# A hybrid transformer layer on one core: the MLP's two matrix products by seven block products of Strassen instead of eight

## The chip, the core and the metric

The kernel runs on one NeuronCore of a Trainium2 chip. TensorE (PE in the profile; PEld is its weight load) multiplies matrices into PSUM, VectorE (DVE), ScalarE (ACT) and GpSimd (POOL) work on elements, and SyncE (SP) issues nearly all DMA transfers, in the order in which they stand in its queue. The metric is the time on the device of one execution, in microseconds (us); smaller is better. Everything is float32. TensorE multiplies float32r operands here, so each float32 product is made of three matmuls on operands that are split into a high part (rounded) and a low part (the rest): high by high, high by low, low by high.

## What is computed

One layer over 2048 tokens of width 1024: a combined input projection, an attention group and a gated group, an output projection with residual, and at the end the squared-ReLU MLP. Only the last two lines are touched by the change:

```python
h = rms_norm(x, norm2_g[l])
f = jnp.square(jax.nn.relu(jnp.einsum('bsd,df->bsf', h, w_ff1[l])))
x = x + jnp.einsum('bsf,fd->bsd', f, w_ff2[l])
```

`h` is 2048 by 1024, `w_ff1` 1024 by 4096, `w_ff2` 4096 by 1024. Each of the two products is, in tiles of 128 by 128 by 512, 1024 tile products, and three matmuls for each: 3072 matmuls, 6144 for both.

## The kernel before

The program has four stages: a first sweep over the 16 token tiles (projections of q, k and v, and row maxima), attention, a second sweep (`sweep2`: the gated group and the output projection, whose sums are the residual that goes to DRAM as four tensors `x1_d`, named x_d in the profile), and `mlp`. All instructions go through a framework that gives each engine a list in an order of its own: it takes them by the order of the program, by the operands that they wait for and by the free buffers of their pools. So two orders matter: that of the source, and that of each engine's list. A pool gives out `bufs` buffers per tag in turn; a tile that takes a buffer waits until its last user is done.

`mlp` works on blocks of 1024 tokens (`TB`), two of them. `prep` loads a tile of 128 rows into `acc` (line 1112, kept for the whole block as the accumulator), squares it on ACT for the norm (line 1115), and transposes it on PE with `ident` (line 246); `split_ps` takes the transposed tile out of PSUM as `hh` (high, ACT line 175) and `hl` (low, DVE line 176), which stay in SBUF for the block. Then it loops over pairs of the 32 column blocks f of `w_ff1` (`CF = 2`). `load_w1` loads a block of 1024 by 128 as `w1r` (line 1071), POOL multiplies it with the norm's gain (line 1072), and `split_sb` makes `w1h` on ACT (line 168) and `w1l` on DVE (line 169). `load_w2` does the same with 128 rows of `w_ff2`. `ff1` multiplies by `gemm3` (lines 205 to 207, one line for each of the three products), applies relu on ACT (line 1096), squares on POOL (line 1097), and splits the result into `fh` and `fl`, which stay in SBUF. `ff2` multiplies these with `w2h`, `w2l` for each of eight token tiles and two halves of the 1024 output columns; DVE multiplies each PSUM bank with the row's 1/rms squared and adds it to `acc` (line 1107). After the last pair of a block `acc` goes to the output.

For the first four tiles of the first block, `prep` alternates with what is left of the second sweep (`rest`), so that PE has work while the tiles are loaded.

Of the kernel before, what the change touches and what calls it, by code (L numbers as in the profile page):

```python
# [8 lines left out]
F32 = mybir.dt.float32  # L9
F32R = mybir.dt.float32r  # L10
AF = mybir.ActivationFunctionType
ALU = mybir.AluOpType
# [51 lines left out]
class InOrder:  # L64
    """An engine whose instructions keep the order in which they are written."""
# [13 lines left out]
class Halves:  # L79
    """Two tiles of four blocks each, indexed as one of eight."""  # L80
# [11 lines left out]
class Engines:  # L92
    """The engines of a core; those named in `pinned` keep the written order."""
# [10 lines left out]
def tile_hybrid_block(  # L104
# [57 lines left out]
    def split_sb(dst_hi, dst_lo, raw, scale=None, on_pool=False):  # L162
        """dst_hi + dst_lo = scale * raw, exactly, with dst_hi rounded to float32r."""
# [14 lines left out]
    def inv_rms(dst, ssq, n):  # L178
        """dst = (ssq / n + eps) ** -0.5"""
        en.vector.tensor_scalar(dst, ssq, 1.0 / n, EPS, ALU.mult, ALU.add)  # L180
        en.gpsimd.tensor_tensor(dst, dst, expo[: dst.shape[0], : dst.shape[1]], ALU.pow)

    def inv_rms_n(pool, dst, ssq, n, name):
        """as inv_rms, by a square root, a reciprocal and a Newton step"""
# [10 lines left out]
    def gemm3(ps, pairs, by_pass=False):  # L195
        """ps = sum over (a_hi, a_lo, b_hi, b_lo) of the three products that float32 needs."""
# [17 lines left out]
    def load_x_t(pool, pst, t, nxt=2, newton=False, tag="tr", xt=None, apart=False, into=None):  # L214
        """x tile, its transposed copy split in two, 1 / rms of its rows."""
# [47 lines left out]
    # additive masks: q by k for the maximum, k by q for the scores (own block, next block)  # L263
# [23 lines left out]
    # ================= sweep 1: q, k, v and the maxima of two branches =================  # L287
    def sweep1():
        if True:
# [87 lines left out]
            def maxima(m, units):  # L377
                """units: (query view, key view, mask, column of m); the masked row maxima."""
# [62 lines left out]
            def behind(t, qn, kn, step):  # L441
                """the part of tile t that trails its projections, in steps between later ones"""
# [26 lines left out]
            def late4(t, n):  # L469
                """a share of the second branch's maxima of the group before"""  # L470
# [58 lines left out]
            def finish(pe, dve):  # L529
                """what is left of the maxima, in two parts"""  # L530
# [9 lines left out]
    # ================= attention: joint softmax over the three branches =================  # L540
    def attention(finish, xnp, xs, tpe, wu):
        with ExitStack() as st:
# [92 lines left out]
            def scores(units, msk, i):  # L635
                """units: (ks, k2, qh, q2 views, width); the exponentials, split in two"""
# [26 lines left out]
            def due(everything=False):  # L663
                """what was put off until some steps had passed"""
# [19 lines left out]
            def head_jobs(h, T):  # L684
# [5 lines left out]
                # d = 1: one bank for 512 queries in order  # L690
# [25 lines left out]
                # d = 4 and d = 16: one bank for each residue mod 4, the query 16 i + 4 c + r in column (c, i)  # L716
# [50 lines left out]
            def first_x(step):  # L767
                """of the next sweep's first tile, the part due at this step"""
# [30 lines left out]
            def weights(step):  # L799
                """of the next sweep's first weights, the part due at this step, counted from the last head"""  # L800
# [48 lines left out]
    # ================= sweep 2: u, g, spatial gating, output projection =================  # L849
# [199 lines left out]
    # ================= squared-ReLU MLP =================  # L1049
    def mlp(pst, late, rest):  # L1050
# [3 lines left out]
        CF = 2  # L1054
        with ExitStack() as st:
            new = lambda name, **kw: st.enter_context(tc.tile_pool(name=name, reuse_waits="tile", **kw))
            cp = new("f1", bufs=1)
            ap = new("f1a", bufs=1)
            rp = new("f1r", bufs=2)
            wps = [new("f1w", bufs=1)]  # L1060
            hh = [cp.tile([P, KD, 512], F32R, name="hh0")]
            hl = [cp.tile([P, KD, 512], F32R, name="hl0")]
            g2 = ap.tile([P, KD], F32, name="g2")
            nc.scalar.dma_start(g2, norm2_g[0].rearrange("(k p) -> p k", p=P))

            def load_w1(f):
# [56 lines left out]
            for t in range(4):  # L1123
                accs.append(prep(0, t))
                if rest:
                    rest.pop(0)()
# [85 lines left out]
```

## Time and profile before

| | |
|---|---|
| median of 3 runs | 2584.57 us (2583.3 to 2596.1) |
| span of the profiled execution, first to last instruction | 2579.8 us |
| what lies around the span, by the median | 4.8 us |
| PE busy | 2534.3 us, 98% of the span |
| DVE, ACT, POOL busy | 51%, 28%, 22% |
| DMA | 209.29 MB, mean 81 GB/s |
| first matmul of the MLP, last matmul's start | 1153.9 us, 2574.7 us |

The time of the profiled execution itself isn't listed apart from its span; the span stands 4.8 us (0.2%) under the median of the runs. The MLP is the stretch from 1153.9 us to the end, 55% of the span. A row of the profile that groups instructions gives line, engine, operation, output and inputs by their names in the program, their shapes, a count, and then the busy time and the mean duration of one in ns. PE's durations are of pipelined matmuls that overlap (about 390 ns each); what one costs in a stream is the distance from start to start. A row of windows gives for each stretch the busy time of each engine with the number of instructions (x), then the granted TensorE clock, the busy share of the DMA engines and what they moved. A row of the timeline gives start, duration, engine, line and operands, and in brackets how long the engine was idle before it and what it waited for.

### The profile page before, as it was taken

The numbers are of one execution on the slowest core, as the hardware profiler recorded it, in microseconds if no ns is written. First come the engines' busy times: TensorE is split into PE (matmuls) and PEld (weight loads), VectorE is DVE, ScalarE is ACT, GpSimd is POOL, SyncE is SP. The second block draws the span as 40 slices with busy tenths as digits, with TensorE's granted clock in tenths as the row PEclk, the third lists the DMA queues.
The fourth block names the chain that finished last, engine by engine and source line by source line (L and its number), as shares of the span: only waits on it lengthen the run. The fifth ranks groups of instructions, "written<-read, shape, count | busy, mean of one in ns | idle before, by whom it ended". The sixth has DMA issues, their size and how long they took to land.

```text
span 2579.8 us, 31560 instructions
## 1 busy us (share of the span) xinstructions
PE 2534.3 (98%) x12052; PEld 2105.5 (82%) x12052; DVE 1322.7 (51%) x2892; ACT 731.7 (28%) x1248; POOL 558.2 (22%) x460
## 2 busy tenths in 40 slices
PE   8999999999988999999999999999999999999999
PEld 6777777999977888878888888888788888888887
DVE  6556656777764444454343444444534444444444
ACT  5222223655662222243212121211322121121210
POOL 1000003555531122122212122221122222121210
PEclk9999996988889999999999999999999999999999
DMA  6434446655542212142111111111321111111111
GB/s 196 107 66 95 95 102 155 176 129 151 182 124 71 74 58 66 58 141 64 57 41 58 41 57 42 49 50 49 127 69 58 42 49 49 49 49 50 49 33 66
DMA packets 189175, 209.29 MB, mean 81 GB/s; under 512 B 16080, under 2 KB 151760, under 8 KB 185296
## 3 DMA queue, kind: packets, MB, share of 16 engines
q1 hardware_dynamic: 180544, 205.67, 27.9%
q10 hardware_dynamic: 8480, 1.60, 0.4%
q8 instruction: 95, 1.56, 0.3%
q14 instruction: 56, 0.46, 0.1%
HBM read 160.19 MB, written 46.99 MB: 80 GB/s over the span
## 4 chain that ended last, share of the span: by engine, by line
PE 94%; DMA 2%; DVE 2%; ACT 1%; issue 1%; POOL 0%; SPq 0%; ACTq 0%; DVEq 0%; POOLq 0%
PE ps_f L205 18%; PE ps_f L206 18%; PE ps_f L207 18%; PE ps_mm L205 8%; PE ps_mm L206 8%; PE ps_mm L207 8%; PE ps_as L74 6%; PE ps_o L74 4%; PE ps_sc L382 2%; PE ps_tr L246 2%; PE ps_mx L74 1%; PE ps_mm L74 1%; PE ps_tr L361 1%; DMA a<-at_d 0%; DMA out_dram<-acc 0%
## 5 line engine op out<-in xcount | busy, mean ns | idle before, releaser
L1107 DVE SCALAR_TENSOR_TENSOR acc<-ps_f,ss,acc 128x512 f32<-128x512 f32 x512 | 378.4, 748 | 231.3 <-PE ps_f L207 231.1
L205 PE MATMUL ps_f<-hh,w1h 128*128 128x512 f32 x1024 | 402.7, 393 | 0.2 <-ACT hh L175 0.2
L206 PE MATMUL ps_f<-hl,w1h 128*128 128x512 f32 x1024 | 402.5, 393 | 0.0
L207 PE MATMUL ps_f<-hh,w1l 128*128 128x512 f32 x1024 | 402.2, 393 | 0.0
L205 PE MATMUL ps_f<-w2h,fh 128*128 128x512 f32 x1024 | 398.8, 389 | 0.0
L206 PE MATMUL ps_f<-w2l,fh 128*128 128x512 f32 x1024 | 398.7, 389 | 0.0
L207 PE MATMUL ps_f<-w2h,fl 128*128 128x512 f32 x1024 | 398.7, 389 | 0.0
L169 DVE TENSOR_TENSOR fl<-relu,fh 128x512 fp32r<-128x512 f32 x128 | 88.6, 692 | 466.1 <-ACT fh L168 466.1
L1072 POOL TENSOR_TENSOR w1r<-w1r,g 128x1024 f32<-128x1024 f32 x64 | 122.5, 1914 | 869.3 <-DMA w1r<-in_w_ff_dram 626.6
L205 PEld LDWEIGHTS ps_f<-hh,w1h 128*128 128x128 f32 x1024 | 192.5, 188 | 43.8 <-ACT hh L175 0.5
L207 PEld LDWEIGHTS ps_f<-hh,w1l 128*128 128x128 f32 x1024 | 192.6, 188 | 43.6
L206 PEld LDWEIGHTS ps_f<-hl,w1h 128*128 128x128 f32 x1024 | 192.5, 188 | 43.0
L205 PEld LDWEIGHTS ps_f<-w2h,fh 128*128 128x128 f32 x1024 | 192.2, 188 | 42.0
L207 PEld LDWEIGHTS ps_f<-w2h,fl 128*128 128x128 f32 x1024 | 192.3, 188 | 40.0
L206 PEld LDWEIGHTS ps_f<-w2l,fh 128*128 128x128 f32 x1024 | 192.2, 188 | 38.8
L1097 POOL TENSOR_TENSOR relu<-relu 128x512 f32<-128x512 f32 x128 | 165.8, 1295 | 242.6 <-ACT relu L1096 242.6
L74 POOL TENSOR_TENSOR pl<-e,ph 128x512 fp32r<-128x512 f32 x144 | 175.5, 1234 | 160.9 <-ACT e L74 122.5
L168 ACT ACTIVATE w2h<-w2r 128x1024 fp32r<-128x1024 f32 x64 | 64.6, 1053 | 510.6 <-PE ps_f L207 508.1
L168 ACT ACTIVATE fh<-relu 128x512 fp32r<-128x512 f32 x128 | 80.9, 632 | 299.9 <-POOL relu L1097 299.9
L74 PE MATMUL ps_o<-ph,v 128*64 128x128 f32 (+3 forms) x816 | 151.1, 272 | 0.9 <-ACT nacc L74 0.9
L74 PE MATMUL ps_as<-qh,ks 128*128 128x256 f32 (+1 forms) x384 | 144.9, 384 | 0.0
L74 PE MATMUL ps_as<-q,k 65*128 65x256 f32 (+1 forms) x384 | 137.1, 369 | 0.0
(254 smaller groups left out, 4234.4 us busy)
## 6 DMA issues: line engine op xcount, KB each, us to landing
w1r<-in_w_ff_dram SPq DMA_DIRECT2D x64, 512.0 KB, 4.5
w2r<-in_w_ff_dram SPq DMA_DIRECT2D x64, 512.0 KB, 3.3
v<-v_d SPq DMA_DIRECT2D x24, 1040.0 KB, 10.4
xt<-in_x_dram SPq DMA_DIRECT2D x32, 512.0 KB, 5.5
v_d<-vt SPq DMA_DIRECT2D x16, 520.0 KB, 6.3
ks<-kt_d SPq DMA_DIRECT2D x16, 512.0 KB, 8.3
x_d<-xt SPq DMA_DIRECT2D x16, 512.0 KB, 2.6
acc<-x_d SPq DMA_DIRECT2D x16, 512.0 KB, 4.4
```

Of the source, the lines that this page charges most:

```text
L74: return self.tc.keep_in_program_order(op(*args, **kwargs))
L168: en.scalar.activation(dst_hi, raw, AF.Copy)
L169: (en.gpsimd if on_pool else en.vector).tensor_tensor(dst_lo, raw, f32(dst_hi), ALU.subtract)
L205: en.tensor.matmul(ps, ah, bh, start=(i == 0), stop=False)
L206: en.tensor.matmul(ps, ah, bl, start=False, stop=False)
L207: en.tensor.matmul(ps, al, bh, start=False, stop=(i == n - 1))
L246: en.tensor.transpose(ps[:, k - k0, :], src[:, k * P : (k + 1) * P], ident)
L361: nc.tensor.transpose(pt[:, j, :], qn[:, j * P : (j + 1) * P], ident)
L382: order[0].matmul(ps[:, j, : mk.shape[1]], qv, kv, start=True, stop=True)
L1072: nc.gpsimd.tensor_tensor(r3, r3, g2.unsqueeze(2).broadcast_to([P, KD, P]), ALU.mult)
L1097: nc.gpsimd.tensor_tensor(r, r, r, ALU.mult)
L1107: nc.vector.scalar_tensor_tensor(acc[:, cs], ps, r2, acc[:, cs], ALU.mult, ALU.add)
```

## The change

Both products are done on operands cut into 2 by 2 blocks, with Strassen's seven products of sums of blocks in place of eight products of blocks. `A_OF`, `B_OF` and `C_OF` say for each product i which blocks are added or subtracted to make its left and right operand, and into which blocks of the result it goes.

- **Norm.** `prep` now applies the norm and its gain before the products: DVE multiplies the rows by 1/rms (line 1094) and takes the transposed tile out of PSUM times the gain (line 1101), as float32 and not split, into `hT`; two DMAs write it to DRAM (`ht_d`, line 1102). 1/rms comes from POOL's power (`inv_rms`).
- **Right operands of the first product.** `h_op` reads blocks of 512 channels by 512 tokens back from `ht_d` (line 1117), DVE adds two of them (line 1120), and `split_sb` makes `bh{i}`, `bl{i}`: seven pairs that stay in SBUF for a block of 1024 tokens, one buffer each. For the second block of tokens the sums are made during the first one and kept in DRAM (`hs_d`, lines 1268 and 1132). The rows, the transposed tiles and the parts of the sums all share one tag, `raw`, of four buffers.
- **Left operands of the first product.** For each of 16 pairs j of column blocks, `load_w1` loads four blocks `w1r` (256 KB each, line 1162); `w_op` makes seven operands: five sums on POOL (tile `as`, line 1105) and seven splits on ACT and DVE (`ah`, `al`).
- **First product.** `ff1` makes seven products of 12 matmuls each (line 1198) in four PSUM banks. Some products accumulate on a bank that has been read already, so that fewer sums are left: DVE does six additions out of PSUM (lines 1209 to 1237), ACT a copy and four relus and squares.
- **Left operands of the second product.** POOL makes five sums of the four result blocks (line 1105, tiles `c`), and seven DMAs of 256 KB (line 1216) write the seven left operands, not split, to DRAM (`s_d`), for each j and each of the two blocks of tokens.
- **Second product.** Seven products in halves of the inner dimension: 14 passes (`passes`), each over 8 steps n. A step reads a left operand of 512 KB from `s_d` into `sr` (line 1304, three buffers), splits it (`s`, four buffers), does 24 matmuls into one bank (line 1316), and DVE adds the bank to one or two of the 16 accumulators `acc` (line 1326), which all stay in SBUF. The right operands `t` of a pass (four tiles; ten buffers) are made during the pass before, from one or two loads of `w_ff2` each (line 1293), a sum on POOL and a split.

```diff
+            def prep(gt):
+                tb, t = divmod(gt, NTB)
+                h = raw()
+                nc.sync.dma_start(h, x1_d[gt // 4][(gt % 4) * P : (gt % 4 + 1) * P, :])
...
+                nc.vector.tensor_scalar(h, h, ss[:, 1:2], None, ALU.mult)
...
+                    nc.vector.tensor_tensor(hT3[:, ks, :], ps, g2[:, ks].unsqueeze(2).broadcast_to([P, 4, P]), ALU.mult)
+                    nc.sync.dma_start(ht_d[tb, kh, t // 4, :, :, (t % 4) * P : (t % 4 + 1) * P], hT3[:, ks, :])
...
+            def h_sum(i, tb, kc):
...
+                        nc.sync.dma_start(r, ht_d[tb, kh, th, :, kc : kc + 2, :])
+                        parts.append(r)
+                if op is not None:
+                    nc.vector.tensor_tensor(parts[0], parts[0], parts[1], op)
+                return parts[0]
...
+            ORDER1 = (3, 2, 1, 5, 4, 7, 6)
+            early = ORDER1[:4]
+            for n, t in enumerate((4, 5, 6, 7, 0, 1, 2, 3)):
+                prep(t)
+                if rest and n % 2:
+                    rest.pop(0)()
+            h_op(ORDER1[0], 0, hop[0])
...
+            def ff1(j, tb, wops):
...
+                            nc.tensor.matmul(
+                                ps[bank], a[:, k, :], b[:, k, :], start=first and k == n == 0,
+                                stop=(k == 3 and n == 2), skip_group_check=True,
+                            )
...
+                for i in (1, 2, 6, 7):
+                    first, second, op = A_OF[i]
+                    dst = c_tile() if i < 3 else f[first]
+                    combine(dst, op, f[first], f[second])
+                    keep(i, dst)
...
+            def s_op(i, half, n):
+                r = sp.tile([P, NH, P], F32, tag="sr", name="sr", bufs=3)
+                nc.sync.dma_start(r, s_d[i, n, :, half * NH : (half + 1) * NH, :])
+                s = sp.tile([P, 2, NH, P], F32R, tag="s", name="s", bufs=4)
+                split_sb(s[:, 0], s[:, 1], r)
+                return s
...
+            def ff2(i, half, n, ts, s):
+                ps = psg.tile([P, 512], F32, tag="f2", name="ps_f2")
+                for k in range(NH):
+                    t = ts[k // 2]
+                    for m, (a, b) in enumerate(((0, 0), (0, 1), (1, 0))):
+                        nc.tensor.matmul(
+                            ps, s[:, a, k, :], t[:, b, k % 2, :], start=k == m == 0, stop=k == NH - 1 and m == 2
+                        )
+                for at, op in C_OF[i]:
...
+                    nc.vector.tensor_tensor(c, c, ps, op)
```

Three places in the engines' lists matter for what follows. The first is PE's list where the second sweep ends. Before, each pair of transposes of `prep` stands between matmuls of the projection, and the MLP's first matmul follows (`ps_mm` is the projection, `ps_tr<-ident,acc` a `prep`):

```order
L206 MATMUL ps_mm<-wol_4_8085,mh 128x512
L246 MATMUL ps_tr<-ident,acc 128x128 x4
L207 MATMUL ps_mm<-woh_4_8069,ml 128x512
L205 MATMUL ps_mm<-woh_5_8070,mh 128x512
L206 MATMUL ps_mm<-wol_5_8086,mh 128x512
```

Now the transposes are those of line 1100, and the last three of the eight tiles stand after all but two of the projection's matmuls, straight ahead of the first product (`ps_f`, line 1198):

```order
L205 MATMUL ps_mm<-woh_3_8076,ah 128x512
L1100 MATMUL ps_tr<-ident,raw 128x128 x8
L206 MATMUL ps_mm<-wol_3_8092,ah 128x512
L207 MATMUL ps_mm<-woh_3_8076,al 128x512
L1100 MATMUL ps_tr<-ident,raw 128x128 x24
L1198 MATMUL ps_f_11782<-bh_11619,ah 128x512
L1198 MATMUL ps_f_11782<-bl_11620,ah 128x512
```

So 24 transposes, of the last three tiles, have moved behind the projection. The second place is SP's list at the same point of the changed program: `raw<-x_d` loads the rows of a tile, `ht_d<-raw` stores a half of a transposed tile, `raw<-ht_d` reads a part of an operand back.

```order
L1102 DMA ht_d<-raw 512x1x128 x4
L996 DMA x_d_71<-xt 128x1024
L1089 DMA raw<-x_d_68 128x1024
L1102 DMA ht_d<-raw 512x1x128 x2
L1162 DMA w1r<-in_w_ff_dram 128x4x128
L1089 DMA raw<-x_d_68 128x1024
L1162 DMA w1r<-in_w_ff_dram 128x4x128 x3
L1102 DMA ht_d<-raw 512x1x128 x2
L1117 DMA raw<-ht_d 128x1024 x2
L1102 DMA ht_d<-raw 512x1x128 x2
L1117 DMA raw<-ht_d 128x1024
```

Where before SP issued seven loads of rows in a row, each load of a tile now stands behind the stores of the tile two before it, whose buffers it takes, and the first reads back stand behind the last stores but one pair. The third place is SP's list in the middle of the first product and at the change to the second: four loads of weights, seven stores of left operands, in turn for each j, and then the first reads of the second product.

```order
L1162 DMA w1r<-in_w_ff_dram 128x4x128 x4
L1216 DMA s_d<-c 128x4x128 x7
L1162 DMA w1r<-in_w_ff_dram 128x4x128 x2
L1216 DMA s_d<-c 128x4x128 x14
L1304 DMA sr<-s_d 128x1024 x5
L1216 DMA s_d<-c 128x4x128 x2
L1304 DMA sr<-s_d 128x1024
L1216 DMA s_d<-c 128x4x128 x5
```

Counted from the start, 4(j+3)+2 weight loads stand ahead of the first store of j through most of the loop (22 ahead of that of j = 2, 26 ahead of that of j = 3): the loads run two j and a half ahead of the stores. In the last rows five reads of `sr` have been moved ahead of the last j's stores.

More of the change, by code (lines that the diff above doesn't have):

```diff
@@ new lines, in w_op @@
+            def w_op(i, block):
+                ah = wp.tile([P, 4, P], F32R, tag="ah", name="ah", bufs=8)
+                al = wp.tile([P, 4, P], F32R, tag="al", name="al", bufs=8)
+                first, second, op = A_OF[i]
+                r = block(first)
+                if second is not None:
+                    r = wp.tile([P, 4, P], F32, tag="as", name="as", bufs=2)
+                    combine(r, op, block(first), block(second))
+                split_sb(ah, al, r)
+                return ah, al
@@ new lines, in mlp, with t_ops @@
+            f1.close()
+            acc_p = new(st, "f2a", bufs=1, side="right")
+            sp = new(st, "f2s", bufs=1)
+            tp = new(st, "f2t", bufs=1)
+            psg = st.enter_context(tc.tile_pool(name="ps_f2", bufs=6, space=PSUM, reuse_waits="tile"))
+            AHEAD = 2
+            ORDER2 = (5, 3, 2, 4, 1, 6, 7)
+            NP = NT // 2
+            NH = NFP // 2
+            accs = {}
+            def t_ops(i, half):
+                first, second, op = B_OF[i]
+                for c in range(half * NH, (half + 1) * NH, 2):
+                    parts = []
+                    for at in (first, second):
+                        if at is not None:
+                            fh, dh = nb(at)
+                            r = raw().rearrange("p (k d) -> p k d", k=2)
+                            src = w_ff2[2 * c * P : (2 * c + 4) * P, dh * 512 : (dh + 1) * 512]
+                            nc.sync.dma_start(r, src.rearrange("(k f p) d -> p f k d", f=2, p=P)[:, fh])
+                            parts.append(r)
+                    if op is not None:
+                        combine(parts[0], op, *parts)
+                    t = tp.tile([P, 2, 2, 512], F32R, tag="t", name="t", bufs=10)
+                    split_sb(t[:, 0], t[:, 1], parts[0])
+                    yield t
@@ new lines, in mlp @@
+            passes = [(i, half) for i in ORDER2 for half in range(2)]
+            steps = [(*p, n) for p in passes for n in range(NP)]
+            ss = [s_op(*steps[0])]
+            ts = list(t_ops(*passes[0]))
+            ss += [s_op(*at) for at in steps[1:AHEAD]]
+            for m, (i, half) in enumerate(passes):
+                nts, more = [], t_ops(*passes[m + 1]) if m + 1 < len(passes) else iter(())
+                for n in range(NP):
+                    at = m * NP + n + AHEAD
+                    if at < len(steps):
+                        ss.append(s_op(*steps[at]))
+                    ff2(i, half, n, ts, ss.pop(0))
+                    nts.extend([t] if (t := next(more, None)) is not None else [])
+                ts = nts
```

247 lines of the change are left out of this document (150 added, 97 removed).

## The prediction

> **What bounds the kernel now.** I read the page's head and its chain of waits first, then windows over the MLP.
>
> ```profile
> span 2579.8 us, 31560 instructions
> PE 94%; DMA 2%; DVE 2%; ACT 1%; issue 1%; POOL 0%; SPq 0%; ACTq 0%; DVEq 0%; POOLq 0%
> 1200.00:1800.00 600.00, 600.00 (x2626) 492.46 (x2625) 165.35 (x224) 31.24 (x53) 1.00 0.15 48
> 1900.00:2500.00 600.00, 600.00 (x2626) 492.44 (x2625) 159.39 (x217) 33.05 (x56) 1.00 0.15 48
> 1153.87 0.50 PE L205 MATMUL ps_f<-hh,w1h 128*128 128x512 f32 x1 [0.25 <-ACT hh L175]
> L207 PE MATMUL ps_f<-w2h,fl x1024: 387/389/476, 1202.6 to 2574.7; 128*128 128x512 f32 x171
> 1800.00:1900.00 100.00, 96.01 (x451) 78.59 (x450) 48.57 (x75) 32.34 (x52) 20.75 (x13) 1.00 0.38 122
> ```
>
> The chain is PE's. The two long windows, of the MLP's tiles alone, show PE without a gap at full granted clock: 600/2626 = 0.2285 us from matmul to matmul. 6144 of them are 1404 us of the 1421 us between the first matmul (1153.9) and the last (2574.7); the rest is 64 transposes, some 6 us, and the change of blocks in the last row. DMA is at 0.15. So in the MLP only the number of matmuls counts, as long as operands come in time.
>
> **What goes: matmuls.** Seven products of eight: first product 32 (j, block) x 7 x 12 = 2688, second 14 passes x 8 steps x 24 = 2688; 5376 in place of 6144. At 0.2285 the 768 are worth 175 us.
>
> **The price of a matmul under more DMA.** The distance isn't the same everywhere. While a `w1r` is landing, and while no DMA runs:
>
> ```profile
> 1501.00:1505.00 4.00, 4.00 (x18) 3.20 (x17) 0.69 (x1) 1.23 (x2) 0.66 (x1) 1.00 0.47 131
> 1501.04 0.40 PE L207 MATMUL ps_f<-hh,w1l 128*128 128x512 f32 x1
> 1503.85 0.39 PE L207 MATMUL ps_f<-hh,w1l 128*128 128x512 f32 x1
> ...
> 1517.00:1521.00 4.00, 4.00 (x19) 3.30 (x19) 2.17 (x4) 0.00 (x0) 0.00 (x0) 1.00 0.00 0
> 1516.82 0.39 PE L207 MATMUL ps_f<-w2h,fl 128*128 128x512 f32 x1
> 1519.54 0.39 PE L207 MATMUL ps_f<-w2h,fl 128*128 128x512 f32 x1
> ```
>
> Each pair of rows is twelve matmuls apart: 2.81/12 = 0.2342, and 2.72/12 = 0.2267. The transfer there runs at 131/0.47 = 279 GB/s of a full set of engines. The change moves far more: 11 DMAs of 256 KB per j are 2.88 MB, 10.3 us of some 19.4 at that rate; a step of the second product reads 512 KB of left operand and 12/7 x 4/8 x 512 KB of weights, 0.97 MB, 3.5 us of 5.5. So transfers run a little over half the time, and I take the middle, 0.2305: 5376 x 0.2305 = 1239 us, with 0.2267 (1219) and 0.2342 (1259) as the ends.
>
> The Trainium skill, page SBUF — State Buffer, section Who interferes with whom, says that a DMA never contends with a compute engine. By that the price would be 0.2267 whatever is moved, 20 us less. The trace doesn't bear it out here: its 0.2342 stands beside a busy DMA.
>
> **Work of the other engines in a j.** Rows by engine, shapes apart:
>
> ```profile
> L169 DVE TENSOR_TENSOR fl<-relu,fh 128x512 fp32r<-128x512 f32 x128 | 88.6, 692 | 466.1 <-ACT fh L168 466.1
> L989 DVE TENSOR_TENSOR xt<-ps_mm,xt 128x512 f32<-128x512 f32 x32 | 22.0, 686 | 26.5 <-PE ps_mm L207 26.5
> L168 ACT ACTIVATE fh<-relu 128x512 fp32r<-128x512 f32 x128 | 80.9, 632 | 299.9 <-POOL relu L1097 299.9
> L1096 ACT ACTIVATE relu<-ps_f 128x512 f32<-128x512 f32 x128 | 75.5, 590 | 191.7 <-PE ps_f L207 191.6
> L74 POOL TENSOR_TENSOR pl<-e,ph 128x512 fp32r<-128x512 f32 x112 | 143.2, 1293 | 137.5 <-ACT e L74 113.2 <-PE ps_o L74 14.9 <-PE ps_as L74 8.8
> L169 DVE TENSOR_TENSOR w1l<-w1r,w1h 128x1024 fp32r<-128x1024 f32 x64 | 79.7, 1245 | 81.6 <-ACT w1h L168 81.4
> L168 ACT ACTIVATE w1h<-w1r 128x1024 fp32r<-128x1024 f32 x64 | 67.8, 1059 | 59.3 <-PE ps_f L206 59.3
> ```
>
> Per j of 84 x 0.2305 = 19.4 us: DVE 7 x 0.69 + 6 x 0.69 = 9.0, ACT 7 x 0.63 + 9 x 0.59 = 9.7, POOL ten sums x 1.29 = 12.9. Per step of 24 x 0.2305 = 5.5 us: DVE 1.25 + half a split 0.62 + 12/7 x 0.69 = 3.0, ACT 1.06 + 0.53 = 1.6. All of it lies beside PE's matmuls, so I cost it at nothing; were that cover gone, POOL's 12.9 a j would be 413 us. Stores wait in SP's list for POOL's last sums, and weight loads are queued behind them; but those loads stand two and a half j ahead of the stores, so a wait of some 8 us there reaches nobody.
>
> **The start of the first product.** Here PE has nothing else to do, and the round trip through DRAM is on the path.
>
> ```profile
> 1137.04 0.63 PE L246 MATMUL ps_tr<-ident,m 128*128 128x128 f32 x4
> 1119.79 0.48 DVE L74 TENSOR_SCALAR m<-m,ms 128x512 f32<-128x512 f32 x1 [0.66 <-POOL ms L181]
> L1115 ACT ACTIVATE hn<-acc 128x1024 f32<-128x1024 f32 x16 | 16.9, 1058 | 15.9 <-DMA acc<-x_d 15.7
> L181 POOL TENSOR_TENSOR ms<-ms,expo 128x1 f32<-128x1 f32 x16 | 9.2, 574 | 178.4 <-DVE ms L180 158.9 <-issue 19.5
> acc<-x_d SPq DMA_DIRECT2D x16, 512.0 KB, 4.4
> x_d<-xt SPq DMA_DIRECT2D x16, 512.0 KB, 2.6
> ks<-kt_d SPq DMA_DIRECT2D x16, 512.0 KB, 8.3
> q<-qt_d SPq DMA_DIRECT2D x8, 512.0 KB, 10.3
> ```
>
> Four `raw` buffers, two for a tile, let two tiles be under way. PE's list puts the first tile's transposes just behind `ps_tr<-ident,m`, so near 1137.5. From then a pair of tiles takes a load 4.4, the square 1.06, the power and its handing over 1.2, the scaling 0.9 (twice 0.48), transposes 1.0, DVE 0.7 and SP's waits for the stores in between, near 10: loads of the third, fifth and seventh tile at about 1139, 1149, 1160, the eighth tile's transposes at 1171, its stores and the read back (4.4) near 1177, add and high part 2.3: the first product starts near 1180 in place of 1153.9, **26 us** late. What is late next are the seven operands: five sums of four reads and two plain ones of two are 24 reads through four buffers, six rounds; a round holds its buffers for landing 4.4, add 1.25, split 1.06 + 1.25, 8.0 in all: 48 us, and with the last product some 50 for the first j in place of 19.4, **31 us** more. PE's list pulls 15 matmuls of the next j ahead, -3. Together **+54**. By the landing of 2.6 (rounds of 6.2, pairs of 8) it would be near 30; by that of 8.3 (rounds of 11.9, pairs of 14) near 90. I take the row nearest in kind, 4.4: the same loads at the same place.
>
> **Two smaller seams.** At the second block of tokens each operand has one buffer, free after its product in the last j and due 16.6 us later (six products of 2.77). The last one's reads stand in SP's list behind the last stores, about 8 us after the last product (add, relu, square, four sums of 1.29); with 4.4 and a split of 2.3 that is 15: just in time, **+2** (0 to 8). Where the second product starts, left operands and weights are split into memory that the last products have just left: four splits of 1.25 on DVE after the fourth and fifth of seven products, **+4** (0 to 12).
>
> **The sum.** Start 1153.9 + 54 + 1239 + 64 transposes 6 + seams 6 + tail 5.1 (2579.8 - 2574.7) = 2464 for the span, and 4.8 around it: **2469 us**. The ends added up give 2425 and 2535; likely not all at once, 2435 to 2510.
>
> **Rivals.** A: the start is hidden and the matmuls cost what they cost now; the whole 175 us come, **2409**. For it: nothing but the short landing; against it the list of PE, with nothing behind the transposes but the products that wait for them. 10%.
>
> B: POOL bounds the first product. Its sums and DVE's subtractions run side by side, and POOL's squares show a spread that could be such a collision:
>
> ```profile
> L1097 POOL TENSOR_TENSOR relu<-relu x128: 1037/1043/1597, 1165.2 to 2532.3; 128x512 f32<-128x512 f32 x128
> ```
>
> Ten at 1.60, a tile's power 0.57 and seven DVE operations of 0.69 in series make 21.4 us a j, 2.0 more than PE's; x 32 = 64 us: **2533**. It decides from 1.9 us a sum; the mean of 1.29 speaks against it. 12%. The Trainium skill, page SBUF — State Buffer, section Who interferes with whom, says that a DVE instruction with two SBUF inputs and a GpSimd one that reads SBUF exclude each other, which is this series; the spread above agrees.
>
> C, the other side: the second product waits for its left operands from DRAM. Three `sr` buffers, each held for a landing and a split of 2.3: a step can't be shorter than (landing + 2.3)/3. At 10.3, the longest median above, it is 4.2, under 5.5; it decides from 14.3, and the whole gain is gone from about 18. At twice 10.3 a step takes 7.6, 2.1 x 112 = 237 more: **2706**. For it: DMA busy over 0.6 with 4 to 8 transfers in the queue; against it the 279 GB/s. 8%.
>
> My forecast has 70%. What a measurement here can't tell from no change is about 0.5%, 13 us. Forecast, A and most of B lie over that on the fast side: faster 0.88, same 0.05, slower 0.07. The range that holds 8 in 10 reaches into A's side and B's: 2425 to 2520.
>
> **What would show it.** Right: 5376 matmuls of the MLP, distance 0.229 to 0.232 in both products; PE idle 45 to 65 us in all between 1140 and 1235, waiting for `raw`, `bh`, `bl`; the first j some 50 us; POOL's sums near 1.3; `sr` landing in 4 to 6. Wrong: PE idle in every j (POOL over 1.9: B), in every step (landing over 14: C), or hardly at the start (A); a distance under 0.228 would say that DMA isn't what stretches it.

## The result

The changed kernel takes 2501.73 us (median of 4 runs, 2491.34 to 2507.25), the kernel before 2587.87 us beside it (4 runs, 2583.3 to 2596.1). The ratio is 0.966, 95% interval 0.963 to 0.970: 3.4% faster. The forecast was 2469 with 2425 to 2520 around it. The time lies inside, 33 us above the forecast, and the terms that make up the difference are not the ones that I was least sure of.

The head of the page of the changed kernel, and windows over its PE, to set beside the 600-us windows of before; the columns of a window are its length, PE busy with its matmuls, granted clock, DMA share, GB/s:

```profile
span 2505.5 us, 31639 instructions
```

```profile
1400.00:1500.00 100.00, 88.96 (x358) 0.93 0.90 265
1500.00:1600.00 100.00, 87.94 (x373) 0.95 0.76 227
1700.00:1800.00 100.00, 100.00 (x443) 1.00 0.54 155
1900.00:2000.00 100.00, 100.00 (x443) 1.00 0.91 326
```

From 1600 on PE is full again in both products: 443 matmuls touch each 100 us, and from start to start one takes 0.2267 us (19.04/84 in the steady j's below), less than the 0.2285 of before although DMA runs at 0.54 to 0.91 instead of 0.15. Between 1196 and 1600 it isn't full. What PE waited for at the start of the MLP (1140 to 1290), in 1250 to 1480, and in 1480 to 1680 (total us, times, longest):

```profile
PE ps_f L1198 <- ACT bh L168: 18.0, 11, 8.8
PE ps_tr L1100 <- DVE raw L1094: 15.3, 5, 5.1
PE ps_f L1198 <- DVE bl L169: 7.3, 7, 1.8
...
PE ps_f L1198 <- ACT c L1206: 7.8, 5, 2.7
PE ps_f L1198 <- DVE c L1209: 2.7, 2, 2.2
...
PE ps_f L1198 <- ACT c L1206: 9.3, 2, 8.3
```

The first three rows are the start, foreseen. The last three are not: there PE waits for a PSUM bank that ACT (line 1206) or DVE (line 1209) has not read yet.

The program is the same up to the end of the second sweep, but that end moves from run to run: the last transposes of `m` (line 246) start at 1137.4 us in the profile of before and between 1134.2 and 1149.6 in the other profiles. So the MLP is compared from those transposes to the end of the last matmul: 1437.7 us before, 1354.1 after, 83.6 less, about the 86 of the medians. In it, counted from the first matmul of each j to that of the next:

| | predicted | measured |
|---|---|---|
| last transposes of `m` to first product | 43 | 48.5 |
| j0 | 50 | 53.7 |
| j1 (with the transposes of a tile) | 17.2 | 22.5 |
| steady j | 19.4 | 19.04 |
| j9, j11 | 19.4 | 27.7, 28.7 |
| j16 (second block of tokens) | 21.4 | 33.9 |
| first product, all 32 j | 656 | 693.7 |
| second product, 112 steps | 623 | 612 |

Steady j's are j8, j12, j14, j15 and all from j17 to j30. The second product's matmuls were 0.2269 us apart before, 3072 x 0.2269 = 697 us; now it takes 612. What is left of the MLP, the start and the first product, took 1437.7 - 697 = 741 us before and takes 1354.1 - 612 = 742 now. So the first product has lost all that its 384 fewer matmuls save, 32 us of it by starting later (48.5 us behind the transposes of `m`, 16.5 before), and **the whole gain is the second product's**.

### The profile page after: what moved, and what is told of

It reads as the page before. It is cut to its first block, busy times and chain, and to the rows that moved or that the text cites. A ratio compares the mean times of both kernels' runs of the same rounds, so it can differ in the third digit from the quotient of the medians.

```text
span 2505.5 us, 31639 instructions
## 1 busy us (share of the span) xinstructions
PE 2395.5 (96%) x11284; PEld 1987.8 (79%) x11284; DVE 1467.7 (59%) x2948; ACT 938.3 (37%) x1540; POOL 844.4 (34%) x644
## 5 line engine op out<-in xcount | busy, mean ns | idle before, releaser
L1316 PE MATMUL ps_f<-t,s 128*128 128x512 f32 x2688 | 611.4, 390 | 2.2 <-DVE c L1237 1.6
L1316 PEld LDWEIGHTS ps_f<-t,s 128*128 128x128 f32 x2688 | 505.3, 188 | 108.2 <-ACT t L168 2.0
L1198 PE MATMUL ps_f<-bh,ah 128*128 128x512 f32 x896 | 360.7, 403 | 44.5 <-ACT bh L168 20.0
L1198 PE MATMUL ps_f<-bl,ah 128*128 128x512 f32 x896 | 358.3, 400 | 8.2 <-DVE bl L169 8.1
L1198 PE MATMUL ps_f<-bh,al 128*128 128x512 f32 x896 | 356.9, 399 | 0.0
L1105 POOL TENSOR_TENSOR as<-w1r 128x512 f32<-128x512 f32 x160 | 218.7, 1374 | 199.5 <-DVE al L169 138.2
L1105 POOL TENSOR_TENSOR c<-c 128x512 f32<-128x512 f32 x160 | 246.3, 1567 | 33.8 <-ACT c L1186 31.7
L1198 PEld LDWEIGHTS ps_f<-bh,ah 128*128 128x128 f32 x896 | 172.8, 193 | 92.6 <-ACT bh L168 27.2
L1198 PEld LDWEIGHTS ps_f<-bl,ah 128*128 128x128 f32 x896 | 172.9, 193 | 47.8 <-DVE bl L169 12.2
L1198 PEld LDWEIGHTS ps_f<-bh,al 128*128 128x128 f32 x896 | 173.1, 193 | 36.1
```

What stands on the lines that cost most here:

```text
L1105: nc.gpsimd.tensor_tensor(dst, a, b, op)
L1198: nc.tensor.matmul(ps[bank], a[:, k, :], b[:, k, :], start=first and k == n == 0, stop=(k == 3 and n == 2), skip_group_check=True,)
L1316: nc.tensor.matmul(ps, s[:, a, k, :], t[:, b, k % 2, :], start=k == m == 0, stop=k == NH - 1 and m == 2)
```

## How a late read stops PE

Timeline of the changed kernel in j9 (start, duration, engine, line; in brackets the idle time before, and what ended it):

```profile
1422.95 2.74 SPq L1216 DMA_DIRECT2D s_d<-c  x2
1423.51 7.21 POOL L1105 TENSOR_TENSOR c<-c 128x512 f32<-128x512 f32 x5
1425.79 0.46 SPq L1117 DMA_DIRECT2D raw<-ht_d  x1
...
1430.48 1.31 DVE L1120 TENSOR_TENSOR raw<-raw 128x1024 f32<-128x1024 f32 x1 [4.61 <-DMA raw<-ht_d]
1431.72 0.68 DVE L1209 TENSOR_TENSOR c<-c,ps_f 128x512 f32<-128x512 f32 x1
1432.45 0.51 PE L1198 MATMUL ps_f<-bh,ah 128*128 128x512 f32 x1 [2.21 <-DVE c L1209]
```

SP's list has two stores of `s_d` ahead of a read of `ht_d`; the read leaves at 1425.79 and lands near 1430.4. DVE's list has the addition that needs it (line 1120) ahead of the subtraction that frees PE's bank (line 1209), so DVE stands still for 4.61 us and PE for 2.21. The waits for ACT go back to the same kind of read, some us earlier in j9:

```profile
1416.11 1.23 DVE L1120 TENSOR_TENSOR raw<-raw 128x1024 f32<-128x1024 f32 x1 [6.90 <-DMA raw<-ht_d]
1417.96 0.60 ACT L1185 ACTIVATE c<-ps_f 128x512 f32<-128x512 f32 x1 [8.08 <-DVE c L1225]
```

An addition waits 6.90 us for its read, DVE's line 1225 stands behind it, ACT's relu waits for that line, and ACT comes so late to its copy (line 1206) that PE waits 2.70 us. And it costs more than the waits. The matmuls around them:

```profile
1425.68 0.50 PE L1198 MATMUL ps_f<-bh,ah 128*128 128x512 f32 x1 [2.70 <-ACT c L1206]
...
1427.05 0.63 PE L1198 MATMUL ps_f<-bh,al 128*128 128x512 f32 x1
1429.61 0.63 PE L1198 MATMUL ps_f<-bh,al 128*128 128x512 f32 x1
```

Behind the wait of 2.70 us the next few matmuls are still 0.23 to 0.34 apart, but from 1427.05 on 0.427 (2.56/6). In the whole first product 48 gaps (among them the transposes of eight tiles) take 62.7 us, and 110 matmuls that are 0.31 to 0.43 apart (81 of them 0.427) add 19.3; with 2.0 at its end that is nearly all of the 84.4 us by which it is longer than 32 steady j's. The Trainium skill, page TensorE: Matmul & The Clock Gate, section Part 1: The HAM clock gate (the "warmup" mystery), gives 426.7 ns for 512 columns on the gated clock, and an idle window of about 3.4 us until the gate closes; the distance agrees, but here waits of 2.2 and 2.7 us were enough. It isn't one length that decides: in e2 below a wait of 3.05 us in j9 is followed by no such matmul.

## The experiments

Each profile was taken once, so parts are compared within profiles, from the marks of the table above. How far these marks move by themselves can be seen from a1 below, which should differ from the changed kernel in nothing that counts here: the whole by 1.5 us, a single j by up to 2.6.

### Stores later in the source (e1)

```diff
                 def keep(i, r):
-                    nc.sync.dma_start(s_d[...], r...)
+                    kept.append((s_d[...], r...))
...
+                store()   # the stores of j-1, on nc.sync
                 x = product("x", 3, True)
```

> The changed kernel with one edit: the seven stores of the sums of j are written into SP's list one j later, ahead of the weight loads of the next j but one, so that no read stands behind a store whose sum POOL hasn't made yet. Theory H (head of SP's list: stores that wait for POOL hold up the reads of `ht_d` and `hs_d` behind them): j9 and j11 fall from 27.7 and 28.7 us to 19.0 to 20.5, j5 to j7 from 20.4 to 22.1 to about 19.5, j16 from 33.9 to 25 or less; the first product from 692 us to about 660; the start (j0 53.7) stays. Rival R (four `raw` buffers are too few there as well): j9, j11 and j16 stay within 3 us of what they were. Rival S (the DVE additions and the splits themselves, and POOL's sums beside them, are the price): the same, they stay.

Measured: j5 to j7 19.9 each (20.4, 20.9, 22.1), j9 21.2, j10 21.2, j11 29.8, j13 19.0 (20.4), j16 31.0; the first product 682.0, transposes of `m` to the last matmul 1340.9, 13.2 us less than the changed kernel. H expected about 660 for the first product and got a third of that fall. And the edit did not do what it says where it mattered: SP's list, as the framework orders it, has the stores and the reads of j9 to j16 in nearly the same order as before. The test had to be made on the list itself (e6 below).

### The sums of the second block at its start (e2)

```diff
-                    elif tb == 0 and j < NTB + 5:
-                        i = [i for i in ORDER1 if B_OF[i][1]][j - NTB]
-                        for kc in range(0, 4, 2):
-                            nc.sync.dma_start(hs_d[i, :, kc : kc + 2, :], h_sum(i, 1, kc))
```

> The changed kernel without the sums made ahead of time: in j8 to j12 nothing is read, added and stored in `hs_d`; the operands of the second block of tokens are made at its start as those of the first are, from two reads and an addition. All theories: j8 to j15 fall to 19.0 to 19.3 (24 us less in j8 to j13). H: j16 then has 24 reads behind the stores in SP's list and takes about what j0 took without its half-speed matmuls, 42 to 50 us instead of 33.9; net 8 to 16 us less. R: j16 is bound by the four buffers, six rounds of 8.0 us, so 48 or more, net 10 less or nothing. S: j16 about 40.

Measured: j9 22.4, j10 to j15 19.0, j8 to j15 together 17 us less; j16 51.6, 17.7 more; the whole 1353.5 against 1354.1. So the two long j's do come from the sums made ahead: all that j11 had too much, and most of it in j9, where the framework has put the first reads for j16 and DVE waits 5.73 us for one. Making the sums ahead is worth nothing: the price only stands at another place. j16 is then as long as R says, not H.

### Six `raw` buffers (e3)

```diff
-                return stg.tile([P, 1024], F32, tag="raw", name="raw", bufs=4)
+                return stg.tile([P, 1024], F32, tag="raw", name="raw", bufs=6)
-... name="c", bufs=14) ... name="w1r", bufs=6) ... name="t", bufs=10)
+... name="c", bufs=12) ... name="w1r", bufs=5) ... name="t", bufs=9)
```

> The changed kernel with six `raw` buffers instead of four (paid for with two `c`, one `w1r` and one `t` buffer). If the four buffers set the pace of the start, as predicted (pairs of tiles, 24 reads in six rounds of 8.0): three tiles are under way at once and there are four rounds, so the first product starts 8 to 14 us earlier (1182 to 1188 instead of 1196, apart from what the attention before it differs) and j0 takes 36 to 42 us instead of 53.7. If what bounds the start is the work in series (landing, square, power, scaling, transposes at half clock, the stores in SP's list): both within 5 us of what they were. H: j9, j11 and j16 stay near 27.7, 28.7 and 33.9; R: they fall to under 22, 22 and 26.

Measured: transposes of `m` to first product 40.8 instead of 48.5, as expected; but j0 51.7, j1 30.8 (22.5), j9 19.5, j10 31.0, j11 26.1, j16 34.3, the whole 1354.7. Two buffers more leave two of the later j's over 25 and j16 as it was, which is not what R expected. The run alone doesn't rule R out, since it has fewer `w1r` and `c` as well, and in j10 POOL waits 10.71 us for weights; e6 below, with four buffers, does for j9 to j11. The timeline of j0 says where the buffers' gain went:

```profile
1187.46 11.77 SPq L1117 DMA_DIRECT2D raw<-ht_d  x9
1199.29 3.04 SPq L1162 DMA_DIRECT2D w1r<-in_w_ff_dram  x3
1207.51 4.46 POOL L1105 TENSOR_TENSOR as<-w1r 128x512 f32<-128x512 f32 x2 [25.10 <-DMA w1r<-in_w_ff_dram]
1210.48 0.80 PE L1198 MATMUL ps_f<-bh,ah 128*128 128x512 f32 x1 [12.12 <-ACT ah L168]
```

With two more buffers nine reads stand ahead of the weights in SP's list; the weights leave at 1199, POOL's sums of them wait until 1207, and PE waits 12.12 us for `ah`. PE's waits for `bh` and `bl` between 1140 and 1290 fall from 25.3 us to 10.8, and waits for `ah` of 14.3 us stand in their place. In j1 PE waits 7.22 us for the transposes of the next tile, whose norm stands behind POOL's sums.

### The first eight tiles ahead (e4)

```diff
+                two = [prep(t, raw0) for t in (4, 5, 6, 7, 0, 1, 2, 3)]   # raw0: 14 buffers, given back before the operands
+                for n in range(3):
+                    next(two[n])              # load, square, scale
+                for n in range(8):
+                    if n + 3 < 8:
+                        next(two[n + 3])
+                    next(two[n])              # transposes, stores
...
```

> The changed kernel with its first eight tiles prepared through fourteen buffers of their own, in memory that the operands take over later, and written in two stages: three tiles are loaded and scaled ahead of the transposes of the first. The four `raw` buffers stay for the operands. If the pace of the tiles (buffers, and the order in which each tile's steps stand behind one another) makes the late start, the first transposes to the first product shrink from 48.8 to 25 to 32 us; j0 stays at 50 to 54. If the work itself binds (DVE 2.6 us a tile, 21 in all; reads back from DRAM), over 40.

Measured: 39.3 instead of 48.5, between the two cases, and j0 53.4. The transposes end at 1171, and then:

```profile
1172.14 6.71 SPq L1119 DMA_DIRECT2D raw<-ht_d  x4
1178.97 0.38 SPq L1173 DMA_DIRECT2D w1r<-in_w_ff_dram  x1
1184.72 0.79 PE L1209 MATMUL ps_f<-bh,ah 128*128 128x512 f32 x1 [13.90 <-ACT ah L168]
```

The same turn as in e3: one weight load leaves at 1179, behind four reads that waited for buffers. The whole is 1346.6, 7.5 us less than the changed kernel.

### Stores on ACT's queue (e5)

```diff
+                for dst, src in kept:
+                    nc.scalar.dma_start(dst, src)   # before the relu of the fourth product of the next j
```

> The changed kernel with one edit: the stores of the seven sums are issued by ACT's queue instead of SP's, in the middle of the next j, when POOL has made the sums, so that SP's list holds no wait for POOL at all. Moving them one j back on SP's own list took j9 from 27.7 to 21.2 but left j11 at 29.8 and j16 at 31.0, because SP reached them just as early. Theory H: j8 to j15 now all within 19.0 to 20.5, j16 25 to 30 (its operands' single buffers and the splits on DVE stay), the first product 692 to 655 to 665 us. Rival S (additions and splits in DVE's and ACT's lists ahead of the banks' readers, whenever the reads land): j11 stays over 25.

Measured: j3 to j11 between 21.8 and 26.4, j16 29.5, j18 24.1; first product 706.6, the whole 1366.8, 12.7 us more. ACT's own waits between 1265 and 1480 (for what, total, times, longest):

```profile
ACT c L1185 <- DVE c L1226: 22.8, 9, 4.9
ACT c L1185 <- DMA s_d<-c: 22.1, 7, 8.1
...
ACT ah L168 <- POOL c L1105: 14.8, 4, 3.7
ACT c L1206 <- POOL c L1105: 10.9, 6, 1.8
```

The framework again took the stores forward, and on ACT they hold up the relus (line 1185), the splits of the weights and the copy that frees a bank (line 1206). So a store that waits for POOL harms the list that it stands in. The marks are S's (j11 26.4, over 25), but this run does not tell H from S for SP: the first row is a wait for DVE, and both kinds wait at once.

### SP's list fixed (e6)

```diff
+            sp[0] = InOrder(tc, nc.sync)      # SP keeps the written order in the first product
...
+                    if tb == 0 and NTB <= j < NTB + 5:
+                        made = [(kc, h_sum(i, 1, kc)) for kc in range(0, 4, 2)]   # reads of ht_d first
+                    block = load_w1((j + 1) % NFP)                                # then the weights
                     ff1(j, tb, wops)                                              # stores of j-1 in it
+                    for kc, r in made:
+                        sp[0].dma_start(hs_d[i, :, kc : kc + 2, :], r)
```

> The changed kernel with SP's list fixed in the first product, from the operands of the first j on. In the two runs that moved the stores in the source only, the framework put them back: SP's list still had stores that wait for POOL ahead of the reads of `ht_d` (and, with the stores on ACT, ACT's list had them ahead of its splits). Now in each j SP has first the reads (the next tile, or four blocks of `ht_d`, and the four weights of the next j), then the seven stores of the j before, then the stores of what DVE made; at the second block of tokens all reads of `hs_d` and `ht_d` stand ahead of the stores of j15. Theory H: j8 to j15 all at 19.0 to 20.0 (in the changed kernel j9 27.7, j11 28.7), j16 20 to 26 instead of 33.9 (its first four reads land during j15), the first product 692 to 650 to 660 us. Rival S (additions and splits in DVE's and ACT's lists): j9 or j11 stay over 25, j16 over 30.

(`InOrder` keeps an engine's instructions in the order of the source.) Measured: j9, j10, j11 19.0 each, j12 19.6, j16 26.6: for j9 to j11 H's marks came true and S's did not, and j16 is 0.6 over H's range. But j5 takes 25.6, j8 27.1, j13 28.3 and j17 29.0, the first product 700.5 where H expected 650 to 660, the whole 1360.9. j8:

```profile
1408.13 2.13 SPq L74 DMA_DIRECT2D raw<-ht_d  x4
1410.32 6.76 SPq L74 DMA_DIRECT2D w1r<-in_w_ff_dram  x4
1417.13 1.23 DVE L1124 TENSOR_TENSOR raw<-raw 128x1024 f32<-128x1024 f32 x1 [9.77 <-DMA raw<-ht_d]
1418.27 0.68 DVE L1217 TENSOR_TENSOR c<-ps_f,c 128x512 f32<-128x512 f32 x1
1419.01 0.80 PE L1202 MATMUL ps_f<-bh,ah 128*128 128x512 f32 x1 [4.97 <-DVE c L1217]
```

(Lines 1124 and 1217 are the addition and a bank's reader.) Now four reads leave together at 1408 and the first pair is there only at 1417; DVE's list has the addition ahead of the bank's reader, as it had in j9 of the changed kernel, and waits. j5 is of this kind too: DVE waits 6.56 us behind the load of a tile's rows. So SP's list set which reads came late in j9 to j11. That a late read stops PE is set by DVE's list, as these rows show (no run changed that list itself).

j13 and j17 are of another kind; no read is late there. j13:

```profile
1510.86 6.68 POOL L1109 TENSOR_TENSOR c<-c 128x512 f32<-128x512 f32 x5 [3.16 <-ACT c L1190]
1519.45 1.08 DVE L169 TENSOR_TENSOR al<-as,ah 128x512 fp32r<-128x512 f32 x1 [5.52 <-ACT ah L168]
1521.19 0.80 PE L1202 MATMUL ps_f<-bh,ah 128*128 128x512 f32 x1 [5.14 <-DVE c L1214]
```

POOL's list has the five sums of results ahead of the next sums of weights (`as`); ACT's split waits 5.81 us for these, DVE's split for ACT's, and the reader of the bank (line 1214) stands behind it in DVE's list. In j17 POOL's five sums take 7.61 us and PE waits 5.51. This is what S names, splits and POOL's sums ahead of a bank's reader: S is out for j9 to j11, not as a whole.

### Tiles ahead and SP's list (f1), and the combination (f2)

f1 joins e4 and e6, with the weights of j0 ahead of the operands' reads.

> The run with SP's list fixed, and the first eight tiles prepared ahead through fourteen buffers as in the run with the tiles ahead. There the transposes ended at 1171, and the first product then stood 13.9 and 11.6 us for `ah`: the weights of j0 stood in SP's list behind reads that waited for buffers. Here they stand ahead of the operands' reads. If SP's list is what holds the start too: the first transposes to the first product 39.6 us there, 30 to 36 here, j0 of 53 to 42 to 48; the whole about 2455 to 2465. If the reads through four `raw` buffers and the additions hold j0: j0 stays at 50 to 54, the whole 2462 to 2472.

Measured: 41.0 to the first product, j0 51.9, j8 24.9, j13 27.4, j16 27.4, j17 28.1; the whole 1351.5, and 2497 us in its one timed run: above both cases. PE's first wait for a product is now

```profile
1181.10 0.79 PE L1209 MATMUL ps_f<-bh,ah 128*128 128x512 f32 x1 [17.17 <-ACT bh L168]
```

for an operand instead of for the weights of e4: with the weights ahead, the reads back are late.

f2 joins e4 and e1 and spreads the sums ahead over j8 to j15:

```diff
+                        for _ in range(2 if j < NTB + 2 else 1):
+                            i, kc = ahead.pop(0)
+                            nc.sync.dma_start(hs_d[i, :, kc : kc + 2, :], h_sum(i, 1, kc))
```

> The version that the runs point to: the changed kernel with the first eight tiles prepared ahead (first transposes to first product 39.6 us instead of 48.8), the stores a j later in the source (j5 to j11 together 8 us less), and the sums of the second block spread: two halves of an operand in j8 and j9, one in each of j10 to j15, so that two reads instead of four pass through the four `raw` buffers in a j. SP's list is left to the framework, since fixing it only moved the waits to j8, j13 and j17. If a late read that DVE's addition waits for is what stops PE (whichever list made it late), fewer reads a j leave fewer stops: j8 to j15 21 us or less each except one, j16 27 to 34, first product 675 to 683 us; the whole 2470 to 2482, against 2585 to 2588 of the kernel before 0.955 to 0.961. If the waits only move again: the first product about 692, the whole 2490.

Measured: 2488.26 us (median of 5 runs, 2482.07 to 2498.15) beside 2584.45 of the kernel before, ratio 0.964, interval 0.962 to 0.966. The start holds (39.6). j9 20.9, j10 22.2, j11 26.9, j12 21.4, j13 27.2, j16 30.8; first product 689.9: the waits only moved again, the expectation's second case. Its profile is 12.7 us shorter than the changed kernel's from the transposes of `m` on, and its median 13 us lower, but the intervals of the two ratios overlap; that f2 is the faster one isn't shown. Nor is it shown that its three edits add up: e1, one of them alone, has 1340.9 by the same marks, f2 1341.4.

### What stretches a matmul (b1, b2, b3, a1)

My price of 0.2305 was the middle of two rates, and I put the higher one down to a transfer. The profile of before has the answer to that already. A window in which the second product runs under a transfer, and its matmuls from the timeline:

```profile
1513.00:1514.00 1.00, 1.00 (x6) 1.00 1.02 328
```

```profile
1512.26 0.39 PE L205 MATMUL ps_f<-w2h,fh 128*128 128x512 f32 x1
1514.30 0.39 PE L205 MATMUL ps_f<-w2h,fh 128*128 128x512 f32 x1
```

Nine matmuls in 2.04 us, 0.2267 each, with all DMA engines busy in the microsecond between. In the first product of before 26 of each 48 matmuls are 231 to 238 ns apart and 22 are 226 to 227, in the same places in every pair of f, transfer or not. Three runs of the kernel before asked what goes with them. b1 exchanges the two pairs of weight tiles:

```diff
-                w1h = wps[f % 2].tile([P, KD, P], F32R, tag=f"w1h{f % 2}", name="w1h")
+                at = f if f < 2 else (f + 1) % 2
+                w1h = wps[at].tile([P, KD, P], F32R, tag=f"w1h{at}", name="w1h")
```

> The kernel before with one edit: from the second pair of f on, the even f's take the two weight tiles that the odd f's had, and the other way round. In the profile of the kernel before, 26 of each 48 matmuls of the first product (the group of the even f and two more) are 231 to 238 ns apart and the other 22 are 226 to 227, in every pair, whether a transfer runs or not. Theory P (the place of the weight tile in SBUF stretches a matmul): the slow ones are now the groups of the odd f, the second 24 of each 48. Theory D (a transfer into SBUF stretches them, as my prediction read it): the slow ones follow the landing of `w1r`, and the matmuls between landings are at 226.7. Theory O (the order: the first group of a pair, whatever its tile): the first 24 of each 48 stay slow. Time within 0.3% of the kernel before by all three.

The first 24 of each 48 stay slow: not P, and not D. (That expectation takes the groups for those of the even f; the list of PE shows that they are those that stream `hh0` and `hl0`, alternating with `hh1` and `hl1`.) b2 moves these tiles by 32 bytes:

```diff
+            cp.tile([P, 8], F32, name="pad")
             hh = [cp.tile([P, KD, 512], F32R, name="hh0")]
...
-            g2 = ap.tile([P, KD], F32, name="g2")
+            g2 = ap.tile([P, 2 * KD], F32, name="g2")[:, 0:KD]
```

> The kernel before with one edit: 32 unused bytes ahead of `hh0`, and 32 more behind `g2`. The slow 24 of each 48 matmuls of the first product are those that stream `hh0` and `hl0`, which start at a multiple of 64 bytes in a partition (17152, 33536); the fast ones stream `hh1` and `hl1`, which start 32 past one (111712, 128096). Now all four start 32 past a multiple of 64, and so does everything behind them. Theory A (the start of the streamed operand against 64 bytes): all 48 at 226 to 227 ns, the MLP 1536 x 7.5 ns = 11 to 12 us shorter. Theory L (the low end of the partition, or anything else of that group, its transfers included): 24 of 48 stay at 231 to 238, time within 3 us of the kernel before.

The same groups stay slow, now at 229 to 237 but for one matmul of 224; 2582.8 us. a1 makes the opposite move in the changed kernel (`g2` twice as long):

> The changed kernel with one edit: 32 unused bytes behind `g2`, so that every operand of the MLP, streamed and stationary, starts at a multiple of 64 bytes instead of 32 past one. Theory A: matmuls go from 226.7 to about 234 ns apart in both products, a steady j from 19.04 to 19.6, a step of the second product by 0.18, the whole 30 to 40 us longer. Theory L: no change of the distance. If only one product gets slower, it isn't the start address alone.

The distance stays at 226.7 in both products, the whole at 1352.6. Theory A is out. b3 multiplies the other half first:

```diff
-                for c in range(TB // 512):
+                for c in reversed(range(TB // 512)):
```

> The kernel before with one edit: each pair of f multiplies the second 512 tokens (`hh1`, `hl1`) ahead of the first (`hh0`, `hl0`). Neither the weight tiles nor the 64-byte start of the streamed operand moved the slow 24 of each 48 matmuls of the first product. Theory L (what the matmul streams: slow ones go with `hh0` and `hl0`): the slow 24 are now the second of each 48. Theory O (the order: the first group after the group of another weight tile or of the second product is slow, whatever it streams): the first 24 stay slow.

Two groups of b3's timeline, the first with `hh1`, `hl1`, the second with `hh0`, `hl0`:

```profile
1501.07 0.39 PE L206 MATMUL ps_f<-hl,w1h 128*128 128x512 f32 x1
1503.79 0.39 PE L206 MATMUL ps_f<-hl,w1h 128*128 128x512 f32 x1
...
1507.21 0.40 PE L206 MATMUL ps_f<-hl,w1h 128*128 128x512 f32 x1
1510.02 0.39 PE L206 MATMUL ps_f<-hl,w1h 128*128 128x512 f32 x1
```

Twelve matmuls each: 2.72 us, then 2.81. The slow ones are now the second 24: theory L. What goes with them is the streamed half `hh0`, `hl0`, in any order and with any weight tile. Why that half streams 3% slower is left open: a pair of the changed kernel's operands (`bh3`, `bl3`) lies where `hl0` lay, and is not slow.

## Why the prediction was right, and where it was wrong

The sign and the number of matmuls held; of the 116 us forecast, 86 came. Rival A is out by the table (the start isn't hidden); of B and C more below. Against the forecast, profile to profile:

- **The price of a matmul: wrong, 20 us too high.** The step "so transfers run a little over half the time, and I take the middle" failed. 5376 x (0.2305 - 0.2267) = 20. The Trainium skill, page SBUF — State Buffer, section Who interferes with whom, says that a DMA never contends with a compute engine, and I set it aside because a slow row stood beside a busy DMA; the 0.2267 at a share of 1.02 above, and 443 matmuls a 100 us at 0.91, agree with the page. My mark for this ("a distance under 0.228 would say that DMA isn't what stretches it") did its work. The two rows that I compared differed in more than the DMA beside them: one is of the first product with `hh`, the other of the second.
- **"A wait of some 8 us there reaches nobody": wrong, 24 us.** I weighed the stores that wait for POOL against the weight loads behind them in SP's list, and not against the reads of `ht_d`, whose additions stand in DVE's list ahead of the readers of the banks. j5 to j13 are 24 us longer than foreseen, 19 of it in j9 to j11, which e2 and e6 tie to these reads.
- **The seam at the second block of tokens, +2 (0 to 8): mis-sized, 14.9.** I had the last operand's reads as just in time. They leave behind seven stores, and the splits of the operands hold up ACT's copy of the first bank before that:

```profile
1579.52 12.04 SPq L1216 DMA_DIRECT2D s_d<-c  x7
1584.39 0.58 ACT L1206 ACTIVATE c<-ps_f 128x512 f32<-128x512 f32 x1
1585.03 0.79 PE L1198 MATMUL ps_f<-bh,ah 128*128 128x512 f32 x1 [8.28 <-ACT c L1206]
1591.65 1.17 SPq L1132 DMA_DIRECT2D raw<-hs_d  x2
1598.09 0.50 PE L1198 MATMUL ps_f<-bh,ah 128*128 128x512 f32 x1 [1.99 <-ACT bh L168]
```

- **The start, +54: right in kind, 15 short.** The first product came 32 us late instead of 26, j0 took 53.7 instead of 50, and j1, which I had 3 us shorter by work pulled ahead, was 3.5 longer than a steady j. Of j0's excess of 34.7, 25.8 are waits and 8.8 come from 46 matmuls at half clock, a term that the sum lacked. PE's waits add up to 42 us between 1140 and 1290, and to 37 in the 1140 to 1235 for which I named 45 to 65. Buffers do set part of the pace up to the first product (e3: 7.7 us less; e4, with another order of steps as well: 9.2). That `raw` alone sets j0 is not borne out: with six buffers j0 is 2 us shorter, and the wait is for the weights.
- **The second product: right.** A seam of some 4 us, as foreseen (1.8 ahead of the first matmul, 2.4 in the first eleven), then no gap. The landing of `sr`, from the DMA issues of the changed kernel's page (count, KB, median us), beside the reads of the first product:

```profile
sr<-s_d SPq DMA_DIRECT2D x112, 512.0 KB, 3.7
raw<-ht_d SPq DMA_DIRECT2D x48, 512.0 KB, 5.3
```

  3.7 us, a little under the 4 to 6 of my mark, is a quarter of the 14.3 from which rival C would decide; `ht_d` took 5.3 for the 4.4 that I reckoned with.
- **POOL's sums "near 1.3": wrong, without effect on the steady j's.** Groups of the changed kernel (count, busy us, mean ns, idle before):

```profile
L1105 POOL TENSOR_TENSOR c<-c 128x512 f32<-128x512 f32 x160 | 246.3, 1567 | 33.8 <-ACT c L1186 31.7 <-DMA s_d<-c 2.1
L1105 POOL TENSOR_TENSOR as<-w1r 128x512 f32<-128x512 f32 x160 | 218.7, 1374 | 199.5 <-DVE al L169 138.2 <-DMA w1r<-in_w_ff_dram 58.2 <-DVE c L1229 2.5
L169 DVE TENSOR_TENSOR al<-as,ah 128x512 fp32r<-128x512 f32 x160 | 156.0, 975 | 85.6 <-ACT ah L168 85.1
```

  1567 and 1374 against 1293, and DVE's `al` 975 against 692. Rival B's collision is there: five sums of each kind are 14.7 us a j. It doesn't decide in the changed kernel, since the steady j's of 19.04 have no gap; e6's j13 and j17 show that POOL's sums can stop PE once the order changes. The Trainium skill, page SBUF — State Buffer, section Who interferes with whom, has a DVE instruction with two SBUF inputs and a GpSimd one that reads SBUF exclude each other; the longer means of both agree.

The differences: start +6, j0 +4, j1 +5, j5 to j13 +24, the seam +13, the second start 0, the matmuls -20; together 32, the distance of this profile from the forecast, both counted from the transposes of `m`. Errors of opposite sign, 52 us too low and 20 too high, make the forecast look nearer than its steps were; that they partly cancel is luck.

## What to carry to other kernels

Price a change that adds reads by the instruction that consumes each read: find it in its engine's list, and look what stands behind it that frees something PE waits for. A reordering in the source, or of one queue, moved such waits here rather than removed them. A saving in matmuls is worth its count only in a stage whose operands come without a wait; here half of the removed matmuls gained nothing, and several waits of some 2 us and more were charged again at half clock.

## What the runs showed of the hardware

- Matmuls of 512 columns in float32r were 0.2267 us apart whatever DMA did, up to a share of 1.02, but for the group of the next point.
- One streamed pair of tiles of the kernel before was 3% slower in every use (0.2342), and moving it, its weights or its turn changed nothing but the pattern within the group.
- Waits of 2.2 and 2.7 us on PE were followed, 1.3 to 1.4 us later, by matmuls 0.427 apart; a wait of 3.05 us in e2's j9 was not.
- The last transposes of `m` came anywhere between 1134.2 and 1149.6 us in fourteen profiles, whose PE instructions up to there differ by four at most; in attention, from 550 to 650 us, the granted clock was 0.90 in the profile of before and 0.72 in that of the changed kernel.
